# Attention of the hybrid layer in another order, with low parts and the gate on w_out's rows on VectorE

## The chip, the cores and the metric

One core of one Trainium2 chip runs the whole program. The metric is the device time of one execution in microseconds. Before the change three runs took 2250.26, 2250.78 and 2255.9 us; the median is 2250.78 us.

The engines are named as in the profile: PE multiplies, PEld loads its weights, DVE and ACT are the vector and the scalar engine, POOL is GpSimd, SP only issues transfers.

## What is computed

256 tokens of width 1024 pass two blocks (feed-forward, a mixing layer, feed-forward) and then one hybrid layer: a normed and modulated input, attention with two kinds of heads, an output product scaled by a gate, and 32 experts of which each token uses 4. The attention, cut to what the change touches:

```python
h = rms_norm_2(x, norm1_g) * (1.0 + scale1) + shift1
proj = h @ w_in                                  # six groups of 512 columns
aq, ak, av, bq, bk, bv = jnp.split(proj, IN_SPLITS, axis=-1)
aq, ak, bq, bk = (rms_norm_2(heads(t), g) for t, g in ...)   # per head of 64
o_a = dilated_mixture_attention(aq, ak, av, alibi_slopes(8)) # 8 heads of 64
# 4 heads, two score sets each, p = softmax(q k^T / 8 - slope * dist):
a = p[:, :, 0] - lam * p[:, :, 1]
o_b = rms_norm_2(a @ bv, diff_norm_g) * (1.0 - lambda_init)
mixed = jnp.concatenate([o_a, o_b], axis=-1) @ w_out
x = x + gate1 * mixed
h2 = rms_norm_2(x, norm2_g) * (1.0 + scale2) + shift2
return x + gate2 * moe_ffn(h2, ...)
```

## The kernel before

Every weight tile of the dense products is split into a high part, rounded by ACT, and a low part, the rest, which DVE subtracts (`split`, L198, tiles `wh` and `wl`). A product is then three: high by high, low by high, high by low.

A feed-forward ends with a "transition": while it finishes its last blocks, it loads and splits the first weights of what follows. There are six of these before the attention's end (`to_ffn` and `columns` in `run`, which pass POOL as the engine of the low parts): ffn1 to mixing and mixing to ffn2 in each layer, ffn2 to the next ffn1, and the last ffn2 to the attention. L329 to L331 make the gated value `gf` and its transpose `gT` for the second product of a feed-forward, L271 to L279 are the layer norm behind it, L868 to L874 the modulated norm `h` in front of the attention. In the mixing, L1763 makes the tile `Ut` which the next step of a recurrence multiplies, and L1785 and L1786 make its output `mix`.

`attention` multiplies the normed input by the six groups of columns of `w_in` (`natural`, 48 products of 128x512 for each, L412 to L414). Group 3 and 4 are q and k of the B heads, 5 their values, 0 and 1 q and k of the A heads, 2 their values. `qk` (L940 to L952) squares a group, sums per head, takes the inverse root by `rstd_wide` (ACT's logarithm and exponential, L236 and L237, and three small DVE operations), multiplies (L944) and transposes (L951, `turn`). `scores` (L967 to L978) makes the scores of one head, adds the bias and takes the maximum (L974), changes its sign (L975), takes exponentials with their sum (L977) and the reciprocal. `a_scores` divides by the sum (L995), `b_scores` combines two sets (L1013 to L1016). `transposed` (L984, L986) transposes the probabilities of one head on PE and copies them by ACT into a tile `eT`; `a_values` and `b_values` call it and multiply by the values at once (L1004, L1023). `b_values` also norms (L1027 to L1032), `b_turn` (L1037 to L1041) transposes the B heads' result.

What runs beside the columns is set by a list: `at(...)` appends a stage, and `beside` takes the next one after each half of `natural` and after each row block of `out_gemm`. Tiles wait for their buffers, and a scheduler may move instructions past each other on their engines where the program's data allow.

`out_gemm` multiplies by the rows of `w_out` (L574, 72 products, and L1082, 24). Before a row block is split, `scaled` multiplies it in place by the gate's row `g1` (L556, on POOL, tile `sq`), which POOL's queue loads (`mod_row`, L834).

The experts' weights, 192 pieces of 2 MB, come through nine slots in a fixed order (`moe_slots`); `prefetch` issues the next piece (L1252). One is issued at the attention's start, two by POOL's queue before `b_values(3)`, five in the route and one behind it. `route` chooses the experts after the attention; the first product of the experts is L1304.

## Time and profile before

| | |
|---|---|
| median of 3 runs | 2250.78 us |
| the profiled execution | 2255.59 us |
| its span | 2253.8 us |
| mean granted TensorE clock | 0.982 |
| PE busy | 2117.4 us (94% of the span) |
| DVE busy | 1094.1 us (49%) |
| ACT busy | 776.3 us (34%) |
| POOL busy | 155.0 us (7%) |
| moved by DMA | 637.66 MB, mean 283 GB/s |

The span runs from the first to the last instruction; the execution's time is a little longer. Busy shares are means over stages that differ: a stage is read from its own stretch, by what its engines waited for. The granted clock is a share of TensorE's full 2.4 GHz, and its lower level, 1.2 GHz, shows as 0.5.

### The profile page before, as it was taken

Reading aid. Unit: us, or ns where it says so; the run is one execution under the profiler, and the core shown is the slowest. Engines: PE = TensorE matmul, PEld = TensorE weight load, DVE = VectorE, ACT = ScalarE, POOL = GpSimd, SP = SyncE. Lnnn points to the kernel's source line nnn. Section 1 sums busy time; section 2 is a strip of 40 time slices with the busy share of each in tenths; the row PEclk is TensorE's granted clock in tenths of the full one; section 3 lists DMA queues with packets and bytes.
Section 4 is the critical chain, followed back from the end, with each engine's and each line's share of the span. In section 5 each row is a group of like instructions: output and inputs, shape, how many; then the busy total and the mean of one; then the engine's idle time right before and its main releaser. Section 6 shows DMA issues by size and latency. Waiting matters only on the chain.

```text
span 2253.8 us, 28233 instructions
## 1 busy us (share of the span) xinstructions
PE 2117.4 (94%) x11564; PEld 1355.5 (60%) x11565; DVE 1094.1 (49%) x1769; ACT 776.3 (34%) x1142; POOL 155.0 (7%) x160
## 2 busy tenths in 40 slices
PE   8999999999999999899989799999999999998997
PEld 7888777888788877688867563333332323232322
DVE  6766966876876686676676732121111111111111
ACT  4555742555455584245547520101010101010100
POOL 0002222000000122200020300000000000000000
PEclk9999998999999999999999799999999999999999
DMA  8765433776675543266554289999999999999996
GB/s 296 262 241 161 140 100 107 263 252 218 209 271 198 174 140 104 94 221 206 180 203 150 108 330 428 427 428 426 427 427 427 428 428 427 427 428 428 427 427 274
DMA packets 194437, 637.66 MB, mean 283 GB/s; under 512 B 25152, under 2 KB 133472, under 8 KB 169728
## 3 DMA queue, kind: packets, MB, share of 16 engines
q1 hardware_dynamic: 177488, 623.82, 70.9%
q0 software_dynamic: 2896, 9.88, 1.2%
q10 hardware_dynamic: 13920, 2.10, 0.5%
q8 instruction: 93, 1.52, 0.3%
q14 instruction: 40, 0.33, 0.0%
HBM read 633.91 MB, written 1.86 MB: 282 GB/s over the span
## 4 chain that ended last, share of the span: by engine, by line
PE 32%; DMA 23%; DVE 4%; ACT 2%; issue 1%; POOL 0%; SPq 0%; ACTq 0%; POOLq 0%
DMA rawm<-in_w_gate_up_dram 14%; PE w L1304 9%; PE w L1327 5%; DMA rawm<-in_w_down_dram 3%; DMA raw<-in_w_gate_up_dram 3%; PE w L161 3%; PE m L337 2%; DMA raw<-in_w_down_dram 2%; PE w L162 2%; PE w L1287 1%; PE w L574 1%; PE w L414 1%; PE w L412 1%; PE w L413 1%; PE w L1331 1%
## 5 line engine op out<-in xcount | busy, mean ns | idle before, releaser
L198 DVE TENSOR_TENSOR wl<-raw,wh 128x1024 fp32r<-128x1024 f32 x332 | 408.1, 1236 | 177.4 <-ACT wh L198 176.4
L198 ACT ACTIVATE wh<-raw 128x1024 fp32r<-128x1024 f32 (+1 forms) x350 | 365.9, 1050 | 328.6 <-PE w L161 109.6
L161 PE MATMUL w<-xT,wh 128*128 128x512 f32 x1328 | 470.5, 396 | 3.6 <-DVE ab L325 3.6
L1304 PE MATMUL w<-rawm,XT 128*64 128x512 f32 x1696 | 387.3, 599 | 22.5 <-DMA rawm<-in_w_gate_up_dram 21.3
L162 PE MATMUL w<-xT,wl 128*128 128x256 f32 x1328 | 374.1, 282 | 0.0
L161 PEld LDWEIGHTS w<-xT,wh 128*128 128x128 f32 x1328 | 250.9, 189 | 63.1 <-DVE ab L325 3.9
L1304 PEld LDWEIGHTS w<-rawm,XT 128*64 128x64 f32 x1696 | 113.9, 137 | 249.9 <-issue 200.8
L162 PEld LDWEIGHTS w<-xT,wl 128*128 128x128 f32 x1328 | 250.3, 188 | 1.6
L337 PE MATMUL m<-wh,gT 128*128 128x512 f32 x592 | 190.9, 393 | 0.0
L1327 PE MATMUL w<-rawm,wh 128*64 128x512 f32 x704 | 164.7, 599 | 14.2 <-DVE wh L1309 10.7
L1345 DVE COPY g<-w 128x64 f32<-128x64 f32 x32 | 7.1, 223 | 330.7 <-ACT PT L1343 330.7
L1352 DVE SCALAR_TENSOR_TENSOR wl<-w,gs,wh 128x512 f32<-128x512 f32 x31 | 23.3, 751 | 221.2 <-PE w L1327 221.2
L337 PEld LDWEIGHTS m<-wh,gT 128*128 128x128 f32 x592 | 111.1, 188 | 26.8 <-issue 1.7
L1327 PEld LDWEIGHTS w<-rawm,wh 128*64 128x64 f32 x704 | 46.3, 136 | 121.8 <-issue 88.8
L337 PE MATMUL m<-wl,gT 128*128 128x512 f32 x296 | 116.3, 393 | 0.0
L1318 ACT ACTIVATE wh<-w 128x512 f32<-128x512 f32 x32 | 19.1, 597 | 277.2 <-PE w L1317 277.2
L414 PE MATMUL w<-wh,xT 128*128 128x512 f32 (+1 forms) x224 | 87.4, 390 | 5.2 <-DVE xT L258 5.2
L1353 ACT ACTIVATE yh<-wl 128x512 fp32r<-128x512 f32 x31 | 19.5, 630 | 208.8 <-DVE wl L1352 208.8
L413 PE MATMUL w<-wl,xT 128*128 128x512 f32 (+1 forms) x224 | 87.3, 390 | 4.4 <-DVE wl L198 4.4
L412 PE MATMUL w<-wh,xT 128*128 128x512 f32 (+1 forms) x224 | 88.8, 398 | 2.5 <-ACT pre L739 1.9
L1304 PE MATMUL w<-raw,XT 128*64 128x512 f32 x352 | 80.3, 598 | 4.2 <-DMA raw<-in_w_gate_up_dram 3.6
L1327 PE MATMUL w<-raw,wh 128*64 128x512 f32 x320 | 75.6, 600 | 8.0 <-DVE wh L1309 5.3
(479 smaller groups left out, 2885.5 us busy)
## 6 DMA issues: line engine op xcount, KB each, us to landing
rawm<-in_w_gate_up_dram SPq DMA_DIRECT2D x104, 2048.0 KB
raw<-in_ffn_w_dram SPq DMA_DIRECT2D x130, 1024.0 KB
rawm<-in_w_down_dram SPq DMA_DIRECT2D x43, 2048.0 KB
raw<-in_w_gate_up_dram SPq DMA_DIRECT2D x22, 2048.0 KB
raw<-in_w_down_dram SPq DMA_DIRECT2D x20, 2048.0 KB
raw<-in_w_in_dram SPq DMA_DIRECT2D x36, 1024.0 KB
adaw<-in_w_ada_dram SPq DMA_DIRECT2D x48, 512.0 KB
raw<-in_w_out_dram SPq DMA_DIRECT2D x12, 1024.0 KB
```

The costliest lines, as they stand in the source:

```text
L161: nc.tensor.matmul(w[:, ab], h[:, k], self.xT[:, k], start=(k == 0), stop=False)
L162: nc.tensor.matmul(w[:, ab, :T], l[:, k], self.xT[:, k, :T], start=False, stop=(k == KD - 1))
L198: made = nc.scalar.activation(h, v, AF.Copy), (low or nc.vector).tensor_tensor(l, v, h.bitcast(F32), op=OP.subtract)
L337: mm = lambda g, w, start, stop: nc.tensor.matmul(acc[t][q], g, w[:, 0, q * 512 : (q + 1) * 512], start=start, stop=stop, skip_group_check ...
L412: self.nc.tensor.matmul(w[:, t, :n], xh, h, start=(k == 0), stop=False)
L413: self.nc.tensor.matmul(w[:, t, :n], xh, l, start=False, stop=False)
L414: self.nc.tensor.matmul(w[:, t, :n], xl, h, start=False, stop=(k == KD - 1))
L574: mm = lambda q, x, w, start, stop: nc.tensor.matmul(acc[t][:, q], x, w[:, 0, q * 512 : (q + 1) * 512], start=start, stop=stop, skip_group ...
L1287: nc.tensor.matmul(wv[:, k], h, at[:, t, lo:hi], start=(n == 0), stop=(n == 3))
L1304: nc.tensor.matmul(gu[c * 64 : c * 64 + 64, b], self.XT[:, k, e * 64 : e * 64 + 64], r[:, j, f0 : f0 + 512], start=False, stop=(k == KD - 1))
L1327: nc.tensor.matmul(td[c * 64 : c * 64 + 64], self.aT[:, s, q], r[:, s, c * 512 : (c + 1) * 512], start=(q == 0 and s == 0), stop=(q == 1 a ...
L1352: nc.vector.scalar_tensor_tensor(self.ms, td, self.gs, self.g2, op0=OP.mult, op1=OP.mult)
```

## The change

1. `scaled` multiplies on DVE instead of POOL.
2. The low parts of the six transitions are left to DVE, as all others.
3. In the attention PE keeps the order of the program (`manual_schedule`). The groups of columns come as 3, 4, 0, 1, 5, 2. Probabilities get a tile for each use and are transposed by `a_turn` and `b_probs_turn` one stage before the products that use them; `eT` gets a fourth buffer. The gate's row is loaded behind group 5.
4. The inverse roots in `qk` and `b_values` are taken by `rstd`: one small DVE operation (L225) and one power on POOL (L227, 128x16 and 128x2).
5. `scores` takes the smallest of the negated scores, and the exponential negates, so that the operation of L975 is gone.
6. One piece of the experts is issued before `b_values(3)` instead of two, and six in the route instead of five; the order of the slots changes in one place.

```diff
--- before.py
+++ after.py
@@ -553,7 +553,7 @@
-            self.nc.gpsimd.tensor_tensor(r[:, j], r[:, j], gain, op=OP.mult)
+            self.nc.vector.tensor_tensor(r[:, j], r[:, j], gain, op=OP.mult)
@@ -908,14 +908,19 @@
-            probs = [quarter(s3, i, 384) for i in range(4)]
-            osq = s3[:, 1536 : 1536 + T]
+            more = ap.tile([P, 384], F32, name="more")
+            probs = [quarter(s3, i, 384) for i in range(5)] + [more] + [quarter(s0, i, 384) for i in range(5)]
+            of_b = lambda hd: (probs[(0, 2, 3, 4)[hd]], probs[(1, 5)[hd % 2]])
+            of_a = lambda hd: probs[(6, 7, 8, 9, 10, 1, 5, 0)[hd]]
+            osq = lambda hd: quarter(s1, 4 + hd, T)
...
             self.prefetch(1)
+            order = self.tc.manual_schedule(engines={mybir.EngineType.PE})
+            order.__enter__()
             w3 = self.natural(None, 512, ahead)
...
-                r = self.rstd_wide(ap, ss, 1e-6, 1.0 / 64)
+                r = self.rstd(ap, ss, 1e-6, scale=1.0 / 64)
...
-            def scores(q, k, rows, p, bias):
+            def scores(q, k, rows, p, bias, s):
...
                 for t, c in parts:
-                    nc.vector.tensor_tensor_reduce(s[:, c], b[:, c], bias[:, c], 1.0, -3e38, OP.add, OP.max, m[:, t : t + 1])
-                nc.vector.tensor_scalar(m, m, -1.0, None, op0=OP.mult)
+                    nc.vector.tensor_tensor_reduce(s[:, c], b[:, c], bias[:, c], -1.0, 3e38, OP.add, OP.min, m[:, t : t + 1])
                 for t, c in parts:
-                    nc.scalar.activation(s[:, c], s[:, c], AF.Exp, bias=m[:, t : t + 1], accum_out=den[:, t : t + 1])
+                    nc.scalar.activation(s[:, c], s[:, c], AF.Exp, scale=-1.0, bias=m[:, t : t + 1], accum_out=den[:, t : t + 1])
...
-                eT = ap.tile([P, 384], F32, tag="eT", name=self.n("eT"), bufs=3)
+                eT = ap.tile([P, 384], F32, tag="eT", name=self.n("eT"), bufs=4)
...
+            def a_turn(p):
+                turned[p] = [transposed(kept["a", 2 * p + c]) for c in range(2)]
+
             def a_values(p):
-                eT = [transposed(kept[2 * p + c]) for c in range(2)]
+                eT = turned[p]
...
+            def b_probs_turn(hd):
+                turned["b", hd] = transposed(kept["b", hd])
+
             def b_values(hd):
-                eT = transposed(kept[hd])
+                eT = turned["b", hd]
...
-                r = self.rstd_wide(ap, ss, 1e-6, 1.0 / P)
+                r = self.rstd(ap, ss, 1e-6, scale=1.0 / P)
...
-            values(5, vb)
-            at((b_scores, 0)), at((b_scores, 1))
             w0 = self.natural([cols(0)], 512)
             qa, turn = qk(0, w0, 0)
-            at((b_values, 0), (b_scores, 2)), at((turn,), (b_values, 1))
+            at((b_scores, 0)), at((turn,), (b_scores, 1))
             w1 = self.natural([cols(1)], 512)
             ka, turn = qk(1, w1, 1)
-            at((b_scores, 3), (b_values, 2)), at((turn,))
+            at((b_scores, 2), (b_probs_turn, 0)), at((turn,), (b_scores, 3), (b_probs_turn, 1))
+            values(5, vb)
+            g1 = self.mod_row(scratch(), 2)
+            at((a_scores, 0), (b_values, 0), (b_probs_turn, 2), (b_values, 1))
+            at((b_probs_turn, 3), (a_scores, 1), (b_values, 2))
             va = values(2, [x[:, 512:] for x in ob])
-            self.prefetch(2, nc.gpsimd)
+            self.prefetch(1, nc.gpsimd)
+            a_turn(0)
             b_values(3)
-            a_scores(0)
+            a_scores(2)
+            a_values(0)
+            a_turn(1)
             b_turn(0)
             b_turn(1)
-            g1 = self.mod_row(scratch(), 2)
+            a_values(1)
             acc = [self.wide() for _ in range(2)]
-            at((a_scores, 1)), at((a_values, 0)), at((a_scores, 2)), at((a_values, 1), (a_scores, 3))
-            at((a_values, 2)), at((a_values, 3))
+            at((a_scores, 3)), at((a_turn, 2)), at((a_values, 2)), at((a_turn, 3)), at((a_values, 3))
...
+            order.__exit__(None, None, None)
@@ -1100,7 +1115,7 @@
-        self.prefetch(5)
+        self.prefetch(6)
@@ -1237,7 +1252,7 @@
-            for name in ("rawE", "xp", "slotp", "raw", "slotp", "raw", "raw2", "slotp", "raw2"):
+            for name in ("rawE", "xp", "raw", "slotp", "raw", "slotp", "raw2", "slotp", "raw2"):
@@ -1518,8 +1533,8 @@
-        to_ffn = lambda l, i: lambda: self.up_ahead(a[f"ffn{i}_w1"][l], a[f"ffn{i}_w3"][l], low=nc.gpsimd)
-        columns = lambda srcs, n: lambda: (None, (x for q in range(2) for x in self.natural_parts(srcs, n, q, nc.gpsimd)))
+        to_ffn = lambda l, i: lambda: self.up_ahead(a[f"ffn{i}_w1"][l], a[f"ffn{i}_w3"][l])
+        columns = lambda srcs, n: lambda: (None, (x for q in range(2) for x in self.natural_parts(srcs, n, q)))
```

The rows below are the engines' orders, before (or with -) and after (or with +), without times; line numbers of the changed kernel are up to 15 higher. First DVE at the transition to the attention, where `h_8550` is the modulated input of the first 128 tokens:

```order
 L872 TENSOR_TENSOR h_8550<-xn_146,row_8546 128x512 x2
+L198 TENSOR_TENSOR wl_10223<-raw,wh_10222 128x1024
+L225 TENSOR_SCALAR rs_e_10195<-mn_s_10193 128x1
+L198 TENSOR_TENSOR wl_10227<-raw,wh_10226 128x1024
+L874 SCALAR_TENSOR_TENSOR h_8550<-h_8550,rs_r_10197,row_8548 128x512 x2
 L271 BN_STATS st_10231<-m_8583 128x6
-L225 TENSOR_SCALAR rs_e_10195<-mn_s_10193 128x1
+L258 TENSOR_TENSOR xT<-m_10203,xT 128x4x128
+L258 TENSOR_TENSOR xT<-m_10210,xT 128x4x128
 L271 BN_STATS st_10231<-m_8584 128x6
-L874 SCALAR_TENSOR_TENSOR h_8550<-h_8550,rs_r_10197,row_8548 128x512 x2
```

Two low parts now stand between the two halves of the modulated norm, and the statistics of the other tokens follow it.

DVE before, around the first L995 and `b_turn` (L1041), where `slot_10277` holds probabilities of the A heads; POOL has eight L556 on its own queue:

```order
L995 TENSOR_SCALAR slot_10277<-slot_10277,st_10996 128x128
L995 TENSOR_SCALAR slot_10277<-slot_10277,st_10996 128x256
L978 RECIPROCAL st_11008<-st_11008 128x2
L974 ISA slot_10277,st_11061<-m_11058,biasA 128x256
L974 ISA st_11061 128x1
L995 TENSOR_SCALAR slot_10277<-slot_10277,st_11008 128x128
L995 TENSOR_SCALAR slot_10277<-slot_10277,st_11008 128x256
L1041 TENSOR_TENSOR slot_10278<-m_11017,slot_10278 128x4x128
L1041 TENSOR_TENSOR slot_10278<-m_11024,slot_10278 128x4x128
L975 TENSOR_SCALAR st_11061<-st_11061 128x2
L974 ISA slot_10277,st_11073<-m_11070,biasA 128x128
```

DVE after at the same place, behind the last group of columns (`m_10869` is a B head's result, `wl_11145` a low part of `w_out`, `m_10940` the scores of the A head 2):

```order
L556 TENSOR_TENSOR raw<-raw,sq_10811 128x1024
L1042 SCALAR_TENSOR_TENSOR h_8550<-m_10888,rs_r_10897,dg 128x128
L1042 SCALAR_TENSOR_TENSOR h_8551<-m_10888,rs_r_10897,dg 128x128
L556 TENSOR_TENSOR raw<-raw,sq_10811 128x1024
L198 TENSOR_TENSOR wl_11145<-raw,wh_11144 128x1024
L977 ISA slot_10276,st_10943<-m_10940,biasA 128x128
L977 ISA st_10943 128x1
L977 ISA slot_10276,st_10943<-m_10940,biasA 128x256
L977 ISA st_10943 128x1
L977 ISA slot_10276,st_10954<-m_10951,biasA 128x128
```

Two of the eight products by the gate and a low part stand ahead of the scores of A head 2.

PE before, behind `b_turn` (`m_11098` and `m_11104` are the transposes of pair 0 of the A heads, `eT_11102` the copy of the first, `w_11033` the first output of `w_out`):

```order
L984 MATMUL m_11098<-ident,slot_10277 128x128 x3
L984 MATMUL m_11104<-ident,slot_10277 128x128 x3
L1004 MATMUL m_11110<-eT_11102,h_8550 64x256
L1005 MATMUL m_11110<-eT_11102,h_8551 64x128
L1004 MATMUL m_11110<-eT_11108,h_8550 64x256
L1005 MATMUL m_11110<-eT_11108,h_8551 64x128
L967 MATMUL m_11136<-slot_10277 128x128
L968 MATMUL m_11136<-slot_10277 128x256
L967 MATMUL m_11148<-slot_10277 128x128
L968 MATMUL m_11148<-slot_10277 128x256
L984 MATMUL m_11176<-ident,slot_10277 128x128 x2
L574 MATMUL w_11033<-wh_11038,slot_10278 128x512
```

PE after, behind the last product of the columns (`m_10979` and `m_10985` are the transposes of pair 0 of the A heads, `eT_10983` the copy of the first, `m_10991` B head 3):

```order
L986 MATMUL m_10979<-ident,slot_10276 128x128 x3
L986 MATMUL m_10985<-ident,slot_10276 128x128 x3
L1033 MATMUL m_10991<-slot_10276,eT_10938 128x128
L1034 MATMUL m_10991<-slot_10276,eT_10938 128x128
L1035 MATMUL m_10991<-slot_10276,eT_10938 128x128
L972 MATMUL m_11004<-slot_10277 128x128
L973 MATMUL m_11004<-slot_10277 128x256
L972 MATMUL m_11015<-slot_10277 128x128
L973 MATMUL m_11015<-slot_10277 128x256
L1011 MATMUL m_11026<-eT_10983,h_8550 64x256
L1012 MATMUL m_11026<-eT_10983,h_8551 64x128
L1011 MATMUL m_11026<-eT_10989,h_8550 64x256
```

In the first, a head's transposes and its values follow each other; in the second, a B head's values and the scores of pair 2 stand between a pair's transposes and its values.

## Rows read from the trace of the kernel before

**Rows 1.** Busy time by stretch (us, busy of PE, PEld, DVE, ACT, POOL; PEclk, DMA, GB/s)

```profile
0.00:1166.30 1166.30, 1108.64 (x6514) 940.56 (x6515) 835.77 (x1212) 593.13 (x816) 134.28 (x148) 0.98 0.56 192
1166.30:1242.70 76.40, 73.30 (x345) 57.52 (x346) 51.09 (x133) 56.14 (x95) 0.00 (x0) 0.98 0.47 164
1242.70:1272.20 29.50, 14.46 (x69) 8.68 (x67) 24.52 (x53) 17.38 (x42) 19.63 (x10) 0.66 0.23 89
1272.20:1303.70 31.50, 31.06 (x143) 23.77 (x144) 18.09 (x47) 11.38 (x27) 0.56 (x1) 0.94 0.55 206
1303.70:1330.00 26.30, 25.55 (x164) 19.75 (x164) 12.76 (x40) 9.70 (x17) 0.55 (x1) 0.81 0.70 259
1330.00:2240.00 910.00, 858.02 (x4304) 302.65 (x4302) 149.28 (x282) 87.01 (x143) 0.00 (x0) 1.00 1.00 422
```

**Rows 2.** Timeline of SP's queue, 1304 to 1335: start, length, instruction

```profile
1317.93 12.17 SPq L1252 DMA_DIRECT2D rawm<-in_w_down_dram  x2
```

**Rows 3.** What PE waited for, 1166 to 1305: us, times, longest

```profile
PE m L984 <- DVE slot L995: 7.3, 4, 2.5
PE m L1023 <- ACT eT L986: 4.6, 3, 1.6
PE w L574 <- DVE wl L198: 4.0, 1, 4.0
PE m L967 <- DVE st L974: 1.9, 1, 1.9
```

**Rows 4.** Timeline of POOL, 1250 to 1275

```profile
1252.52 18.58 POOL L556 TENSOR_TENSOR raw<-raw,sq 128x1024 f32<-128x1024 f32 x8 [7.70 <-DMA sq<-mods]
```

**Rows 5.** DVE's groups, 1250 to 1275: busy us, mean ns

```profile
L995 DVE TENSOR_SCALAR slot<-slot,st 128x128 f32<-128x128 f32 (+1 forms) x8 | 9.9, 1277 | 0.0
L975 DVE TENSOR_SCALAR st<-st 128x2 f32<-128x2 f32 x5 | 5.5, 1096 | 0.0
L198 DVE TENSOR_TENSOR wl<-raw,wh 128x1024 fp32r<-128x1024 f32 x2 | 4.4, 2222 | 0.0
```

**Rows 6.** Timeline of DVE, the same operations undisturbed

```profile
1250.09 0.16 DVE L975 TENSOR_SCALAR st<-st 128x2 f32<-128x2 f32 x1
1251.82 0.55 DVE L995 TENSOR_SCALAR slot<-slot,st 128x128 f32<-128x128 f32 x2
1272.97 1.21 DVE L198 TENSOR_TENSOR wl<-raw,wh 128x1024 fp32r<-128x1024 f32 x1
```

**Rows 7.** Timeline of PE, two successive products in full flow

```profile
1240.87 0.39 PE L413 MATMUL w<-wl,xT 128*128 128x512 f32 x1
1241.10 0.39 PE L414 MATMUL w<-wh,xT 128*128 128x512 f32 x1
```

**Rows 8.** ACT's groups by form, 1166 to 1305

```profile
L236 ACT ACT_TABLE_LOAD x7 | 9.0, 1283 | 0.1
```

**Rows 9.** POOL's groups by form, whole span

```profile
L227 POOL TENSOR_TENSOR rs_r<-rs_e,mhalf 128x8 f32<-128x8 f32 x4 | 6.6, 1657 | 26.1 <-DVE rs_e L225 26.1
```

**Rows 10.** Timeline of DVE, last ffn2 into attention

```profile
1143.86 3.55 DVE L279 SCALAR_TENSOR_TENSOR xn<-y,rs_r,ln_b 128x512 f32<-128x512 f32 x2
1147.33 3.43 DVE L872 TENSOR_TENSOR h<-xn,row 128x512 f32<-128x512 f32 x2
1150.69 0.68 DVE L271 BATCH_NORM_STATS2 st<-m 128x6 f32<-128x512 f32 x1
1158.13 1.29 DVE L872 TENSOR_TENSOR h<-xn,row 128x512 f32<-128x512 f32 x2
```

**Rows 11.** What PE waited for, 1120 to 1167

```profile
PE m L252 <- DVE h L874: 6.2, 2, 6.0
PE m L337 <- ACT gT L330: 1.5, 1, 1.5
```

**Rows 12.** What PE waited for, 340 to 600

```profile
PE m L337 <- ACT gT L330: 2.7, 1, 2.7
```

**Rows 13.** What PE waited for, 900 to 945 (second mixing into ffn2)

```profile
PE m L1767 <- DVE Ut L1763: 1.7, 1, 1.7
```

More of the change, by code (lines that the diff above doesn't have):

```diff
@@ L968, in scores @@
                 nc.tensor.matmul(b[:, P:384], q[rows, p, P:T], k[rows, p, 0:T], start=True, stop=True)
-                s = probs.pop(0)
-                probs.append(s)
                 st = ap.tile([P, 4], F32, tag="st", name=self.n("st"), bufs=8)
@@ L992, in a_scores @@
                 for hd in (2 * p, 2 * p + 1):
-                    s, den = scores(qa, ka, slice(hd % 2 * 64, hd % 2 * 64 + 64), p, self.biasA[:, hd])
+                    s, den = scores(qa, ka, slice(hd % 2 * 64, hd % 2 * 64 + 64), p, self.biasA[:, hd], of_a(hd))
                     for t, cs in parts:
                         nc.vector.tensor_scalar(s[:, cs], s[:, cs], den[:, t : t + 1], None, op0=OP.mult)
-                    kept[hd] = s
+                    kept["a", hd] = s
+            turned = {}
+            def a_turn(p):
+                turned[p] = [transposed(kept["a", 2 * p + c]) for c in range(2)]
             def a_values(p):
-                eT = [transposed(kept[2 * p + c]) for c in range(2)]
+                eT = turned[p]
                 o = self.bank()
@@ L1010, in b_scores @@
             def b_scores(hd):
-                s0, d0 = scores(qb, kb, slice(0, 64), hd, self.biasB[:, hd])
-                s1, d1 = scores(qb, kb, slice(64, 128), hd, self.biasB[:, hd])
+                s0, d0 = scores(qb, kb, slice(0, 64), hd, self.biasB[:, hd], of_b(hd)[0])
+                s1, d1 = scores(qb, kb, slice(64, 128), hd, self.biasB[:, hd], of_b(hd)[1])
                 nc.vector.tensor_scalar(d1, d1, nlam, None, op0=OP.mult)
@@ L1016, in b_scores @@
                     nc.vector.scalar_tensor_tensor(s0[:, cs], s1[:, cs], d1[:, t : t + 1], s0[:, cs], op0=OP.mult, op1=OP.add)
-                kept[hd] = s0
+                kept["b", hd] = s0
+            def b_probs_turn(hd):
+                turned["b", hd] = transposed(kept["b", hd])
             def b_values(hd):
-                eT = transposed(kept[hd])
+                eT = turned["b", hd]
                 o = self.bank()
@@ L1026, in b_values @@
                 oc = slice(hd * P, (hd + 1) * P)
-                nc.scalar.activation(osq, o[:, :T], AF.Square)
+                nc.scalar.activation(osq(hd), o[:, :T], AF.Square)
                 ss = ap.tile([P, 2], F32, tag="oss", name=self.n("oss"), bufs=2)
-                nc.vector.tensor_reduce(ss, osq.rearrange("p (t i) -> p t i", t=2), AX.X, OP.add)
-                r = self.rstd_wide(ap, ss, 1e-6, 1.0 / P)
+                nc.vector.tensor_reduce(ss, osq(hd).rearrange("p (t i) -> p t i", t=2), AX.X, OP.add)
+                r = self.rstd(ap, ss, 1e-6, scale=1.0 / P)
                 for t in range(2):
```

## The prediction

> **What bounds the kernel now.** I read the table by stretches first [rows 1]. From 1330 to 2240 us the DMA share is 1.00 at 422 GB/s: the weights of the 32 experts stream in, in 192 pieces of 2 MB. Nothing before that fills the DMA (0.47, 0.23, 0.55 in the attention, 0.70 in the route). So the end hangs on when the stream begins without a break. Nine pieces are issued ahead; the row of the last of them [rows 2] holds two issues, and the second one, the tenth piece, ends at 1330.1: it needs a buffer which the first expert's products give free, and these follow the route, 26 us after the attention's last product (L1082, 1303.7). From there to the end nothing changes. Hence the rule of this prediction: a microsecond of the attention, or of anything before it, is one of the end, as long as the nine pieces have landed when the first expert wants them.
>
> Before 1166 PE is busy 1108.6 of 1166.3 us at a granted clock of 0.98 [rows 1]: PE is the bound there, and only its waits can be had. The attention is three stretches [rows 1]: A (1166.3 to 1242.7, the columns of `w_in`; PE busy 73.3 of 76.4), B (to 1272.2, from the last of these columns to where `w_out`'s products run without a break; PE busy 14.5 of 29.5, DVE 24.5, the granted clock 0.66, between the two levels of 2.4 and 1.2 GHz) and C (to 1303.7; PE busy 31.1 of 31.5).
>
> The chain of PE's waits in there [rows 3] names DVE's L995 (7.3 us), its low part L198 (4.0) and L974 (1.9), all in B, and ACT's L986 (4.6 in three waits, two of them in A).
>
> **Why B is slow.** POOL multiplies `w_out`'s rows by the gate from 1252.5 on, eight in a row, 18.6 us, after 7.7 us of waiting for the gate's row [rows 4]. In that time DVE's operations that read SBUF last several times what they last elsewhere: eight L995 9.9 us, five L975 5.5, two L198 4.4 [rows 5]; undisturbed a pair of L995 takes 0.55, an L975 0.16, an L198 1.21 [rows 6]. So 9.9 - 2.2, 5.5 - 0.8 and 4.4 - 2.4 is lost: 7.7 + 4.7 + 2.0 = 14.4 us of DVE's 24.5. L974, which reads PSUM and one SBUF tile, is not drawn out.
>
> The Trainium skill's page "SBUF — State Buffer", section "Who interferes with whom", says that a DVE instruction with two SBUF inputs, or in a two-port mode, contends with a GpSimd instruction that reads SBUF, and that the second to come blocks for the whole of the other. The stretched L198 and L995 agree with it; by the page the whole 14.4 us would go with the move to DVE, as by the rows.
>
> **The change, part by part.**
>
> *Gate on DVE.* POOL's 18.6 us go. DVE takes eight operations of the shape of L198 (128x1024, two SBUF inputs), so 1.21 each [rows 6], 9.7 in all. By the order, two of them stand before the end of the last columns, ahead of a low part that those need; three in B and three in C. The gate's row is now requested behind w1's power, by my setting of the order some 15 us before the end of A, and the low part behind the first gate is wanted some 10 us after that; today's load costs POOL 7.7 us of waiting [rows 4], so it fits, by little.
>
> *B after.* DVE's own work there: 24.5 - 14.4 = 10.1; plus three gates (3.6), plus low parts, of which the order has three in B where one and a half stood (1.8), less the scores of heads 0 and 1 that move into A (about 1.7): 14 us. The order also has a chain: PE's first products of head pair 0 wait for ACT's copy of the transposed probabilities, which stands behind ACT's exponentials of pair 1, which wait for DVE's L974 of pair 1, which stands behind two gates and a low part. That chain costs waits that are not DVE work; I put 4 us on it. B after is 18 us (from 14, DVE without a wait, to 24.5, all of DVE's busy time of now), a gain of 11.5 (5 to 15.5).
>
> *C after.* The 96 products of `w_out` (8 row blocks, 2 x 2 outputs, 3 terms) at 0.23 us (two successive starts [rows 7]) are 22 us, with the last scores, transposes and values of the A heads, some 4 us, 26. Today it is 31.5 with a first part at the lower clock and the 4.0 us wait in front of it as B's last [rows 3]. If the clock is down at the start, because PE waits in B, some 1.5 us come on top: 27.5, a gain of 4.0 (1.5 to 5.5).
>
> *A after.* The two L986 waits (3.1 of 4.6) arise as ACT does two table loads for each root, 14 in the attention, 1.28 us each for L236 [rows 8] and as many for L237, with the copy behind them. The root is now one POOL power per use. For the 128x16 case the trace has only 128x8, at 1.66 us [rows 9]: between that and twice it, 3.3; I take 3. DVE's product L944 waits for it, as it now waits for ACT's two loads, two functions and three small DVE operations (about 3.5), so the wait itself is no longer than before. Behind L944 stand low parts for the next columns; the last one comes a little late for w0 and w1 (0.4 us each, by setting the order against 11.2 us of products). Into A move the transposes of w1's columns and the scores of pair 0, about 2 us of PE work that B loses. So A gains 3.1 - 0.8 - 2.0, near 0.5 (a loss of 1 to a gain of 3). Program order on PE changes nothing there: its columns ran in that order already.
>
> *The smaller edits.* Sixteen L975 (0.16 us undisturbed) leave DVE; hidden behind PE everywhere but B, and counted there. More buffers for probabilities and a fourth eT take no time. One piece fewer is fetched before the end of the attention and one more by the route: by the order of SP's queue five pieces then follow from about 1270 on, 4.9 us each at the stream's 422 GB/s, the last before the route needs it. Free, covered by the DMA's share of 0.55 in C [rows 1]; 4.9 us if the cover fails.
>
> *Low parts of the six transitions.* At the step to the attention, POOL's low parts draw L279 out to 3.55 us a pair and L872 to 3.43, where a pair of L872 takes 1.29 later [rows 10]; with L279 taken as like it, 4.4 us go. PE's wait for `gT` there (1.5 [rows 11]) goes as well. Against it: two low parts of 1.21 now stand between L872 and L874, and two L271 (0.68 [rows 10]) follow L874 that lay beside POOL's work. 1.5 + 4.4 - 2.4 - 1.4: a gain near 2.0. At the step from ffn2 to the next ffn1 the wait for `gT` (2.7 [rows 12]) is down to about 0.6: 2.1. At each step from mixing to ffn2 a low part now stands in front of L1786 and so of `Ut` (L1763), for which PE waits 1.7 us [rows 13]: it waits 1.2 us longer, twice, a loss of 2.4. The steps from ffn1 to mixing (576 columns) have room. Net 1.7 (a loss of 2.4 to a gain of 5).
>
> **Sum.** 0.5 + 11.5 + 4.0 + 1.7 = 17.7 us. The profiled execution takes 2255.6 (span 2253.8), the median of the three runs is 2250.78 and two of them lie at 2250.3 and 2250.8, so the profiled one is 4.8 above. The gain is the same for both: 2237.9 on the profiled one's scale, 2233 on the median's.
>
> **The rivals.**
>
> *B's chain stays as long.* DVE has 9.7 us more to do and PE now may not go past a late instruction. If B lasts 29.5 and C starts as cold as now, only A and the transitions gain: 2250.8 - 2.2 = 2248.6, no change. For it: the chain above crosses ACT and DVE three times. Against it: it needs 15 us of waits beside 14 of work.
>
> *The powers lock DVE.* By the page's rule above, POOL's power reads SBUF and would block a low part (two SBUF inputs) as the gate does now. By the rows, the price is a power's length each time a low part stands between the root's input and L944. The order shows that once (w1) of four times, since L944 mostly follows at once: 3.3 us; if all four block, 13.2. 2236 to 2246. Against it: three of the four have only L944 behind them, which waits for its power in any case.
>
> *A piece comes late.* With one piece fewer ahead the first experts catch up with the DMA: 4.9 us, 2238. Against it: 26 us of route at a share of 0.70.
>
> *Slower: the columns run at the lower clock.* The last low part of w0, w1 and w2 stands behind a DVE product that waits for a power. If that wait grows to several microseconds in front of each, PE idles as in B, and there the granted clock was 0.66. At 1.2 GHz 48 products take 11.2 us more. Three times that is 33.6: 2233 + 33.6 = 2267. It turns the gain into a loss over 0.3% once 2.2 of the three are cold (17.7 + 6.8 = 24.5 over 11.2). Against it: A's clock is 0.98 with waits of 1.6 us in it [rows 1, 3].
>
> **How the numbers follow.** Forecast 0.66 (own range 2222 to 2241), chain as long 0.13, powers 0.06, late piece 0.09, cold columns 0.06. A difference under 0.3%, 6.8 us, is about what cannot be told from none. Faster needs less than 2244.0: 0.66 less 0.02, 0.09, 0.05 of the powers, and 0.05 of the first rival, where only C gains: 0.83. Within: 0.11. Slower: 0.06. The range of 2219 to 2247 leaves out most of the first rival and the cold columns above, and at the low end what B and the transitions would bring together at their bounds.
>
> **What would show it.** After: no POOL instruction of 128x1024; L995 pairs at 0.55 throughout; no table loads between `exp` calls; B (from the last column product to unbroken `w_out` products) near 18 us, C near 27.5, A near 76; two waits for `Ut` of 2.9; PE's wait for h (L874) near 3 where it is 6.2 [rows 11]; the first expert's tenth piece issued 17 to 18 us sooner. It is wrong if B is above 25, if a low part behind L944 holds PE over 2 us in A, or if the stream of weights starts with a gap.

## The result and the profile after

The changed kernel takes 2226.14 us, the median of four runs (2224.84 to 2233.84), against 2250.79 for four of the kernel before: 0.9893, 95% interval 0.9866 to 0.9919, so 24.6 us or 1.1% less. Forecast were 2233, a range of 2219 to 2247, and faster at 0.83. Direction and range hold; the gain is 7 us larger than the sum.

Single runs of one kernel lie up to 16 us apart here (11 of the kernel before, on one chip: 2247.6 to 2263.4). So below the lengths of stretches are compared, with medians beside them: A, B and C together last 115.4 and 114.7 us in two profiles of the changed kernel, 137.2 in that of before and in that of E3, whose attention is the same.

The profiled execution takes 2226.42 us, its span 2224.6. The busy table by stretch, cut where [rows 1] is cut, with the same columns:

```profile
0.00:1162.00 1162.00, 1110.51 (x6514) 942.48 (x6515) 842.41 (x1230) 592.65 (x816) 99.11 (x129) 0.98 0.56 192
1162.00:1238.40 76.40, 75.61 (x357) 59.42 (x358) 54.62 (x124) 43.95 (x82) 15.33 (x7) 0.96 0.43 145
1238.40:1250.10 11.70, 8.73 (x68) 6.22 (x66) 11.12 (x41) 9.40 (x30) 1.98 (x3) 1.00 0.85 325
1250.10:1277.30 27.20, 26.92 (x134) 20.50 (x133) 16.81 (x38) 10.14 (x22) 0.56 (x1) 1.00 0.65 249
1277.30:1300.50 23.20, 22.48 (x163) 17.22 (x163) 12.94 (x41) 9.71 (x17) 0.56 (x1) 0.93 0.79 298
1300.50:2210.00 909.50, 857.48 (x4301) 302.48 (x4298) 149.40 (x282) 87.00 (x143) 0.00 (x0) 1.00 1.00 423
```

Against [rows 1]: the attention begins at 1162.0 instead of 1166.3. A lasts 76.4 as before, though with PE busy 75.6 of it instead of 73.3. B lasts 11.7 instead of 29.5, with the clock at 1.00 instead of 0.66. C lasts 27.2 instead of 31.5. The route, here 23.2 instead of 26.3, is the same code; its clock was 0.81 before and is 0.93 now. That difference is scatter: from the attention's last product to the first one of the experts (L1304 before, L1319 after) it is 21.2 us before and 18.0 after, but 17.9 and 18.1 in E9 and E3, whose attention is as slow as before, and 17.8 to 20.1 in all others. From there to the last work of the engines it is 923.1 us before and 923.2 after. What PE waited for, 1120 to 1305 (to compare with [rows 3, 11]):

```profile
PE m L252 <- DVE h L874: 5.0, 2, 3.1
PE w L414 <- DVE xT L258: 2.0, 1, 2.0
PE m L986 <- DVE h L1042: 0.9, 1, 0.9
PE m L1033 <- DVE st L977: 0.8, 1, 0.8
PE m L972 <- ACT eT L988: 0.7, 1, 0.7
```

Of the four waits in [rows 3] none over 0.9 us is left; what stays at the attention's begin is 2.0 for xT, and the wait for h (L874) has gone from 6.0 to 3.1 at its longest. DVE's groups inside B now:

```profile
L198 DVE TENSOR_TENSOR wl<-raw,wh 128x1024 fp32r<-128x1024 f32 x2 | 2.4, 1220 | 0.0
L556 DVE TENSOR_TENSOR raw<-raw,sq 128x1024 f32<-128x1024 f32 x2 | 2.4, 1218 | 0.0
L997 DVE TENSOR_SCALAR slot<-slot,st 128x128 f32<-128x128 f32 (+1 forms) x6 | 1.5, 312 | 0.0
```

L198 and the gate's L556 take 1.22 us each, one after the other on DVE, and L997 (before: L995) 0.31 where it took 1.28 in [rows 5]. DVE is busy 11.12 of B's 11.70 us, ACT 9.40 and PE 8.73: by busy time DVE is the nearest to the limit now.

### The profile page after: what moved, and what is told of

Same layout as the page of the kernel before. It is cut to its first block, busy times and chain, and to the rows that moved or that the text cites. A ratio compares the mean times of both kernels' runs of the same rounds, so it can differ in the third digit from the quotient of the medians.

```text
span 2224.6 us, 28162 instructions
## 1 busy us (share of the span) xinstructions
PE 2108.9 (95%) x11564; PEld 1351.2 (61%) x11565; DVE 1089.9 (49%) x1755; ACT 754.4 (34%) x1112; POOL 117.5 (5%) x141
## 4 chain that ended last, share of the span: by engine, by line
PE 33%; DMA 26%; DVE 3%; ACT 1%; issue 0%; POOL 0%; SPq 0%; ACTq 0%; POOLq 0%
DMA rawm<-in_w_gate_up_dram 14%; PE w L1319 8%; DMA rawm<-in_w_down_dram 5%; PE w L1342 5%; DMA raw<-in_w_gate_up_dram 4%; PE w L161 3%; PE m L337 2%; DMA raw<-in_w_down_dram 2%; PE w L162 2%; PE w L574 1%; PE w L1302 1%; PE w L414 1%; PE w L413 1%; PE w L412 1%; PE w L1346 1%; PE m L1378 1%
## 5 line engine op out<-in xcount | busy, mean ns | idle before, releaser
L198 DVE TENSOR_TENSOR wl<-raw,wh 128x1024 fp32r<-128x1024 f32 (+1 forms) x350 | 422.8, 1216 | 187.8 <-ACT wh L198 186.9
L198 ACT ACTIVATE wh<-raw 128x1024 fp32r<-128x1024 f32 (+1 forms) x350 | 366.3, 1051 | 346.4 <-PE w L161 113.3
L1319 PE MATMUL w<-rawm,XT 128*64 128x512 f32 x1536 | 351.1, 599 | 20.9 <-DMA rawm<-in_w_gate_up_dram 19.9
L1319 PEld LDWEIGHTS w<-rawm,XT 128*64 128x64 f32 x1536 | 103.1, 137 | 222.0 <-issue 179.4
L1342 PE MATMUL w<-rawm,wh 128*64 128x512 f32 x848 | 197.6, 599 | 15.5 <-DVE wh L1324 12.0
L1342 PEld LDWEIGHTS w<-rawm,wh 128*64 128x64 f32 x848 | 55.7, 136 | 142.5 <-issue 102.7
L1319 PE MATMUL w<-raw,XT 128*64 128x512 f32 x512 | 116.7, 598 | 5.7 <-DMA raw<-in_w_gate_up_dram 5.0
L1319 PEld LDWEIGHTS w<-raw,XT 128*64 128x64 f32 x512 | 34.3, 136 | 76.2 <-issue 61.8
```

The source lines that it names most:

```text
L198: made = nc.scalar.activation(h, v, AF.Copy), (low or nc.vector).tensor_tensor(l, v, h.bitcast(F32), op=OP.subtract)
L1319: nc.tensor.matmul(gu[c * 64 : c * 64 + 64, b], self.XT[:, k, e * 64 : e * 64 + 64], r[:, j, f0 : f0 + 512], start=False, stop=(k == KD - 1))
L1342: nc.tensor.matmul(td[c * 64 : c * 64 + 64], self.aT[:, s, q], r[:, s, c * 512 : (c + 1) * 512], start=(q == 0 and s == 0), stop=(q == 1 a ...
```

## The experiments

Lengths in us, from the start of products in each profile: A from the first column product behind the wait for xT to the end of the last one, B and C together from there to the end of the last product of `w_out`. In E11 that wait is gone, so only B and C can be set beside the others. The medians in the first two rows are those of the result.

| kernel | A | B + C | sum | median | ratio to before, 95% |
|---|---|---|---|---|---|
| before | 76.4 | 60.8 | 137.2 | 2250.8 | |
| after | 76.4 | 39.0 | 115.4 | 2226.1 | 0.9893 (0.9866 to 0.9919) |
| E1 before, gate on DVE | 76.3 | 51.1 | 127.4 | 2246.7 | 0.9972 (0.9957 to 0.9987) |
| E2 after, gate on POOL | 78.9 | 46.0 | 124.9 | 2237.0 | 0.9919 (0.9900 to 0.9937) |
| E3 before, low parts on DVE | 76.4 | 60.8 | 137.2 | 2249.4 | 0.9975 (0.9960 to 0.9989) |
| E4 after, low parts on POOL | 74.7 | 39.0 | 113.7 | 2234.3 | 0.9906 (0.9885 to 0.9926) |
| E5 after, again | 75.2 | 39.5 | 114.7 | 2230.2 | 0.9872 (0.9848 to 0.9897) |
| E6 after, roots by ACT | 76.1 | 48.4 | 124.5 | 2235.8 | 0.9913 (0.9888 to 0.9938) |
| E7 after, PE free | 76.1 | 40.5 | 116.6 | 2228.3 | 0.9866 (0.9838 to 0.9893) |
| E8 after, five pieces in the route | 74.9 | 40.3 | 115.2 | 2226.7 | 0.9871 (0.9845 to 0.9896) |
| E9 before, roots by POOL | 76.1 | 60.6 | 136.7 | 2257.5 | 1.0011 (0.9999 to 1.0023) |
| E10 before, all but the order | 76.0 | 49.2 | 125.2 | 2236.2 | 0.9932 (0.9910 to 0.9955) |
| E11 after, L822 later | | 39.0 | | 2222.7 | 0.9867 (0.9845 to 0.9888) |

Beside E1 to E4 the kernel before had a median of 2254.6, beside E5 to E8 2257.8, beside E9 to E11 2254.4.

**E1, E2: the gate's products.** The edit, in the kernel before and reversed in the changed one:

```diff
-            self.nc.gpsimd.tensor_tensor(r[:, j], r[:, j], gain, op=OP.mult)
+            self.nc.vector.tensor_tensor(r[:, j], r[:, j], gain, op=OP.mult)
```

> The kernel before, with the eight products by the gate (L556) on DVE and nothing else changed. Theory (POOL's products block DVE): the stretch B, 29.5 us before, loses the 14.4 us by which DVE's operations were drawn out and takes on some four products of 1.2 us, so it lasts 18 to 21 us, and the median goes from 2250.8 to about 2241. Rival (the order of transposes and values makes B long, not the block): B stays above 26 us and the median within 3 us of 2250.8.

> The changed kernel, with the eight products by the gate back on POOL and nothing else. Theory of the block: DVE's operations with two SBUF inputs beside them are drawn out to 2 to 4 us again, B goes from 11.7 to above 20 us and the median from 2226 to 2235 or more. Rival (the new order alone hides them): B stays under 15 us, the median within 3 us of 2226.

With the gate on DVE the attention is 9.8 us shorter in the old order (E1); with it on POOL it is 9.5 longer in the new one (E2). The median of E1 falls by 7.9, where 10 were expected, and its rival (within 3) falls. In E1 no single stretch can be set against B's forecast, since products of `w_out` and waits alternate there; B and C together lose 9.7. E2's rival falls too: its ratio stands 0.0026 and 0.0047 behind the two of the changed kernel (E5 is the second), 6 to 11 us. Its first product of `w_out` starts 19.4 us behind A's end, just short of the 20 expected, and 2.5 of its 9.5 us lie in A, where POOL now begins. E2's POOL (one row of eight products), then DVE's groups beside it:

```profile
1222.93 21.52 POOL L556 TENSOR_TENSOR raw<-raw,sq 128x1024 f32<-128x1024 f32 x8 [3.64 <-DMA sq<-mods]
```

```profile
L997 DVE TENSOR_SCALAR slot<-slot,st 128x128 f32<-128x128 f32 (+1 forms) x12 | 11.2, 983 | 0.1
L198 DVE TENSOR_TENSOR wl<-raw,wh 128x1024 fp32r<-128x1024 f32 x4 | 7.0, 1746 | 3.4 <-ACT wh L198 3.4
```

L997 is back at 0.98 on average instead of 0.31, L198 at 1.75 instead of 1.22. While POOL multiplies, each tensor_scalar of DVE takes about as long as one of POOL's products, some 2.3 us. The prediction says this of DVE's operations that read SBUF, but it isn't so for all of them: the reduction L1039 and the reciprocal L980 read SBUF too and keep their 0.40 and 0.14 us. DVE in E2, two rows of its timeline and one of its groups while POOL multiplies (1223 to 1244.4):

```profile
1233.22 9.03 DVE L997 TENSOR_SCALAR slot<-slot,st 128x128 f32<-128x128 f32 x4
1242.17 2.30 DVE L225 TENSOR_SCALAR rs_e<-oss 128x2 f32<-128x2 f32 x1
```

```profile
L1039 DVE TENSOR_REDUCE oss<-slot 128x2 f32<-128x256 f32 x2 | 0.8, 400 | 0.0
```

POOL's eight products last 21.5 us there, and 18.6 in [rows 4]: five take 2.3 to 2.4 us each, as all eight do before, and three take 3.2 to 3.4. That fits DVE holding POOL up too. What PE waited for in E2:

```profile
PE m L972 <- DVE h L1042: 6.6, 1, 6.6
PE m L1033 <- DVE st L977: 3.0, 1, 3.0
```

The longest, 6.6 us, is for the B heads' result (L1042), not for probabilities. Behind it are two causes that E2 doesn't separate: the L225 above, the input of that head's root, is held until 1244.5, and the root's power stands behind the eight products on POOL's own queue, which end at 1244.5 as well. E1 takes the attention's roots on ACT, so its 9.8 us are those of the products alone.

**E3, E4: the low parts of the transitions.**

```diff
-        to_ffn = lambda l, i: lambda: self.up_ahead(a[f"ffn{i}_w1"][l], a[f"ffn{i}_w3"][l], low=nc.gpsimd)
+        to_ffn = lambda l, i: lambda: self.up_ahead(a[f"ffn{i}_w1"][l], a[f"ffn{i}_w3"][l])
...
-        columns = lambda srcs, n: lambda: (None, (x for q in range(2) for x in self.natural_parts(srcs, n, q, nc.gpsimd)))
+        columns = lambda srcs, n: lambda: (None, (x for q in range(2) for x in self.natural_parts(srcs, n, q)))
```

> The kernel before, with the low parts of the six transitions on DVE and nothing else. The two profiles show the attention begin 4.4 us sooner after the change (1162.0 for 1166.3): theory, the transitions give 3 to 5 us, the median is 2246 to 2248. Rival, the prediction's own sum: 1.7 us, 2249. A third: the two runs merely differ, and the transitions give nothing.

> The changed kernel, with the low parts of the six transitions back on POOL and nothing else. Theory: the attention begins near 1166 again, the median is 2229 to 2231, and PE's wait for Ut falls back to 1.7 us while that for h (L874) rises from 3.1 to 6. Rival, the prediction's own sum: 2228. A third: no difference from 2226.

E3 gains 5.2 us on the medians (2.5 to 9.0 by its interval), so the forecast of 1.7 just falls, and so does "nothing". E4's ratio stands 0.0013 and 0.0034 behind the two of the changed kernel, 3 to 8 us, but the intervals overlap. Its waits are as expected, 1.7 for `Ut` and 6.0 for h. Its attention begins at 1167.3 where the changed kernel's begins at 1162.0, but this begin scatters: 1155.1 to 1166.0 in the nine profiles with these low parts on DVE (1165.1 in E3), 1166.3 to 1169.3 in the four with them on POOL.

Where the gain comes from is seen by setting the same PE products of the profiles side by side. At the step to the attention, between 1130 and 1155, all nine profiles with these low parts on DVE gain 4.7 to 5.4 us on the profile of before, and E1, E4 and E9 nothing; by the second half of the first columns some 3 are left. At the step from ffn2 to the next ffn1, between 550 and 600, eight of the nine gain 1.1 to 1.7 (E8 loses 1.0), and E1, E4 and E9 lose 1.6 to 3.3. At the step from mixing to ffn2 the wait for `Ut` rises as forecast, 340 to 600 in the profile after:

```profile
PE m L1782 <- DVE Ut L1778: 3.0, 1, 3.0
PE m L337 <- ACT gT L330: 1.0, 1, 1.0
```

3.0 for the 1.7 of [rows 13], the same at both such steps, and `gT` 1.0 for the 2.7 of [rows 12]. But within 40 us the lateness at the first `Ut` is given back: between 345 and 400 the shift against before changes by -0.8 in the changed kernel and in E3, by -0.9 in E1 and E4, whose low parts are on POOL (-1.8 to 1.3 in the other profiles with them on DVE, -3.1 in E9). At the second one, between 920 and 945, profiles with the low parts on DVE fall back by 0 to 1.2 us, the one after by 3.0, and E1, E4 and E9 by 0.9, -1.2 and 0.8. So of the loss of 2.4 in the sum about 1 may be there, and it can't be told from scatter.

**E5: the changed kernel again.**

> The changed kernel itself once more, beside the kernel before, since runs of one kernel lie up to 10 us apart here. Theory: the stretches A, B and C together last 115.4 us again (before 137.2), and what scatters lies in the mixing, in the route and where the experts' stream begins; the median is 2222 to 2230 with before at 2250 to 2255.

114.7 for 115.4, and 2230.2 at the upper end of the range, beside 2257.8 for the kernel before, above its own. The ratio repeats (0.9872 for 0.9893). The experts' part, from its first product to the last work of the engines, lasts 927.7 in this profile and 923.2 in the first one: 4.5 us of scatter that the change doesn't make, since E9, with the old attention, has 928.7.

**E6: the roots by ACT again.**

```diff
-                r = self.rstd(ap, ss, 1e-6, scale=1.0 / 64)
+                r = self.rstd_wide(ap, ss, 1e-6, 1.0 / 64)
...
-                r = self.rstd(ap, ss, 1e-6, scale=1.0 / P)
+                r = self.rstd_wide(ap, ss, 1e-6, 1.0 / P)
```

> The changed kernel, with the inverse roots of the attention by ACT's logarithm and exponential again (two table loads each) and nothing else. Theory (the loads hold up the copies and the exponentials behind them on ACT): A gains 2 to 4 us and B, whose chain crosses ACT three times and holds four roots, 2 to 5; the median rises by 4 to 9 over the changed kernel. Rival, the prediction's sum: a root by ACT takes 3.5 us where a power takes 3, so A and B together rise by no more than 2, as the transposes now stand a stage ahead.

9.1 us more, all of it in B and C, none in A: the place of the theory is half right, and B, 9.6 longer than after, is above its upper bound of 5. The median is 5.7 above that of E5 beside it, inside the theory's 4 to 9, and the rival falls. The row of B in E6's busy table, and ACT's loads for the logarithm inside it:

```profile
1231.20:1252.50 21.30, 13.85 (x68) 10.36 (x66) 13.57 (x58) 18.71 (x42) 0.53 (x1) 0.68 0.54 197
```

```profile
L236 ACT ACT_TABLE_LOAD x3 | 3.8, 1283 | 0.1
```

B lasts 21.3 us with ACT busy 18.7 of them, and with as many loads at L237 six loads take 7.7 us. DVE is busy 13.6. With the roots by ACT it is ACT that is nearest to the limit in B, as without them it is DVE; and the granted clock is 0.68, about as in B before (0.66).

**E7: PE in the scheduler's order.**

```diff
-            order = self.tc.manual_schedule(engines={mybir.EngineType.PE})
-            order.__enter__()
...
-            order.__exit__(None, None, None)
```

> The changed kernel without the program's order on PE: the scheduler may again move PE's instructions. Theory (the order in which the steps are written makes the gain): A, B and C stay within 2 us of 115.4 together and the median within 3 us of the changed kernel. Rival (program order keeps products from standing in front of late probabilities): transposes and values slip among the products of w_out again, B or C grow by 4 us or more.

116.6 for 115.4, and no ratio that tells them apart: holding PE to program order is worth nothing that these runs show. What is left of part 3 of the change is the order in which the steps are written, with its buffers.

**E8: the pieces ahead.**

```diff
-        self.prefetch(6)
+        self.prefetch(5)
```

> The changed kernel, with five pieces of the experts' weights issued in the route instead of six, so eight ahead in all. Theory (the pieces ahead are covered, the stream's end hangs on the first buffer that comes free): the next piece is issued by the experts' first steps and the time from the first expert's product to the end stays at 923 us, the median within 3 us. Rival (each piece ahead is worth its own 4.9 us on a full DMA): 4 to 5 us more.

The time from the first expert's product to the end is 923.3. The edit took no piece away, though: the experts' first step asks for it, at 1283.46 by SP's timeline, seven microseconds after the attention's end, where the changed kernel issues it right at that end:

```profile
1283.46 0.52 SPq L1267 DMA_DIRECT2D rawm<-in_w_gate_up_dram  x1
```

What it shows is that a piece may come that much later at no cost, not what a missing one costs.

**E9, E10: the roots in the old order, and everything but the order.** E9 is the kernel before with E6's edit reversed; E10 has that, E1's edit and E3's.

> The kernel before, with the inverse roots by POOL's power and nothing else (the gate's products stay on POOL). Theory (in the old order B ends with POOL's eight products whatever the roots do): the roots gain the 3.1 us of PE's waits in A at most, A, B and C together go from 137.2 to 133 or more. Rival (the roots are worth the same 9 us in either order): 128, and the median 9 us below the kernel before.

> The kernel before, with the gate on DVE, the low parts on DVE and the roots by POOL's power, but the old order of groups, transposes and buffers. If the parts add up (gate 9.6, roots 9.1 of the 21.8 us), A, B and C together last 118 us, 3 more than in the changed kernel, and the order is worth 3 us. Rival (the new order is what lets the others pay): 124 or more. A third: the order is worth nothing, 115.

E9 gains 0.5 us in the attention and nothing in time: the first theory. POOL's eight products and DVE's groups beside them, in E9:

```profile
1256.20 19.64 POOL L556 TENSOR_TENSOR raw<-raw,sq 128x1024 f32<-128x1024 f32 x8 [4.31 <-DMA sq<-mods]
```

```profile
L995 DVE TENSOR_SCALAR slot<-slot,st 128x128 f32<-128x128 f32 (+1 forms) x8 | 10.7, 1374 | 0.0
L198 DVE TENSOR_TENSOR wl<-raw,wh 128x1024 fp32r<-128x1024 f32 x3 | 6.5, 2167 | 0.0
```

As long as POOL blocks DVE, the unbroken products of `w_out` start behind POOL's last one, and the loads taken off ACT buy 0.5 us. E10 lasts 125.2, as long as E6 and E2: the parts do not add up, and the rival holds. What PE waited for in E10:

```profile
PE m L1023 <- ACT eT L986: 4.2, 2, 2.7
PE w L414 <- DVE xT L258: 2.8, 1, 2.8
PE w L574 <- DVE w L264: 1.5, 1, 1.5
PE m L1004 <- ACT eT L986: 1.1, 1, 1.1
```

With gate and roots moved, the old order still has products that wait for ACT's copy of the transposes right in front of them (L1023, L1004: 5.3 us, of which 2.7 in A), and B and C lose 10.2 against the changed kernel. These waits are the smaller part of it. B and C as one stretch, in E10 and after:

```profile
1235.80:1285.00 49.20, 42.33 (x210) 29.79 (x209) 36.12 (x101) 25.61 (x62) 3.07 (x5) 0.97 0.40 144
1238.40:1277.30 38.90, 35.65 (x200) 26.72 (x199) 27.94 (x77) 19.55 (x51) 2.54 (x4) 1.00 0.71 272
```

Behind the columns the old order has 8.2 us more of DVE's work, 6.1 of ACT's and 6.7 of PE's busy time, and 3.6 more in which PE is idle. In A the changed kernel has 6.0 us more of DVE's work than E10 (54.6 for 48.6): the new order moves work from behind the columns to beside them, where PE is busy anyway. E10 differs from the changed kernel in the small edits too (sixteen L975 of 0.16 us, the pieces of the experts, PE's program order), so the 9.8 us are the order's with these. The order alone in the kernel before was not run.

**E11: an edit that the profile after suggests.** In front of the second half of the first columns DVE has L822, a product that nobody needs until the route, and waits there for a transfer (DVE's timeline after):

```profile
1160.09 1.23 DVE L822 SCALAR_TENSOR_TENSOR row<-row,sq 128x1024 f32<-128x1024 f32 x1 [2.13 <-DMA row<-mods]
1161.23 1.28 DVE L258 TENSOR_TENSOR xT<-m,xT 128x512 fp32r<-128x512 f32 x2
```

```diff
-        self.nc.vector.scalar_tensor_tensor(A, A, 1.0, scratch, op0=OP.add, op1=OP.mult)
+        made = self.nc.vector.scalar_tensor_tensor(A, A, 1.0, scratch, op0=OP.add, op1=OP.mult)
+        if name == "norm2_g_2":
+            self.tc.keep_in_program_order(made)
...
+            next(gain2)
             kb, turn = qk(4, w4, 3)
             at(), at((turn,))
-            next(gain2)
```

> The changed kernel, with the product L822 (the second norm's row, which waits for a transfer) kept behind the low parts of the first columns on DVE, where the profile shows it 2.1 us waiting in front of the last xT. Theory: PE's wait of 2.0 us for xT goes and the second half of the first columns starts 2 to 3 us sooner, so 2 to 3 us off the changed kernel's median. Rival: the wait moves to the power of the first root, behind which L822 now stands, and nothing is gained.

The same operations in E11, then the power beside L822:

```profile
1158.60 1.36 DVE L258 TENSOR_TENSOR xT<-m,xT 128x512 fp32r<-128x512 f32 x2 [0.71 <-ACT xT L257]
1168.22 1.22 DVE L822 SCALAR_TENSOR_TENSOR row<-row,sq 128x1024 f32<-128x1024 f32 x1
```

```profile
1168.40 3.83 POOL L227 TENSOR_TENSOR rs_r<-rs_e,mhalf 128x16 f32<-128x16 f32 x1 [9.70 <-DVE rs_e L225]
```

xT (L258) starts at 1158.6 instead of 1161.2. The granted clock from 1160 to 1170, after and in E11:

```profile
1160.00:1170.00 10.00, 8.03 (x22) 6.29 (x23) 4.97 (x6) 3.18 (x3) 0.00 (x0) 0.59 0.10 43
```

```profile
1160.00:1170.00 10.00, 10.00 (x45) 8.04 (x44) 7.41 (x11) 6.07 (x6) 1.60 (x1) 1.00 0.52 158
```

From the start of the second tokens' L872 (L874 in E11; 1153.7 and 1153.6) to the end of the attention it is 123.8 us after and 118.4 in E11, 5.4 less, and 4.9 less than in E5 (123.3). Of the 5.4, 2.9 lie in front of the second half of the columns, where the wait was, and 2.6 in A, whose clock stayed at its upper level instead of 0.59. Its median is the lowest of the study (2222.7), but E7's ratio (0.9866) is as low as its 0.9867, and its interval overlaps those of the changed kernel, so as a time it is not shown to be faster. The rival's wait is there, and hidden: the power next to L822 takes 3.8 us instead of 2.9.

## Why the prediction was right, and by how much its terms were not

**What bounds the kernel.** Right. The experts' part lasts 923.2 us for 923.1, and the end moved by what the attention and the stages before it gained (26 us in these two profiles), with the scatter of the route (3 us) on top. The tenth piece is issued at 1300.4 instead of 1329.7, so the stream moved as the end did, by 29 us in these two profiles.

**A** (gain 0.5, bounds -1 to 3): 0.0 in these two profiles. The waits for L986 are gone (3.1), and PE is busy 2.3 us more with the work that moved in. Part of A is how long the clock stays at its lower level behind the wait for xT, and that scatters between two profiles of the changed kernel. The first ten microseconds of A, after and in E5, where the wait is 2.8 us:

```profile
1162.00:1167.00 5.00, 5.00 (x12) 3.94 (x13) 1.74 (x2) 1.42 (x2) 0.00 (x0) 0.50 0.00 0
1167.00:1172.00 5.00, 5.00 (x22) 3.94 (x21) 3.32 (x7) 3.56 (x4) 0.00 (x0) 0.88 0.36 109
1162.10:1167.10 5.00, 5.00 (x15) 3.96 (x16) 1.88 (x3) 2.12 (x2) 0.00 (x0) 0.66 0.00 0
1167.10:1172.10 5.00, 5.00 (x24) 3.98 (x23) 4.45 (x8) 3.04 (x3) 0.00 (x0) 1.00 0.53 174
```

In E5 A lasts 75.2 us, a gain of 1.2.

**B** (gain 11.5, bounds 5 to 15.5): 17.8, outside the bounds. This is the mis-sized term, 6.3 us. The forecast had 14 us of DVE work and 4 us of waits in the chain over ACT; measured are 11.1 of work, since two products by the gate and two low parts lie in B where three of each were counted, and 0.6 of DVE's idle time. The 4 us of waits for the chain were not there. What was wrong below the number is its cause. The sum gave nearly the whole gain of B to the gate's products, and put the roots into A and at nothing in B. E1 and E2 show 9.6 for the gate; E6 shows 9.1 for the roots, in B, where ACT otherwise spends 7.7 us in loads; E10 shows 9.8 for the order with the small edits. Each of the three, taken out of the changed kernel, leaves the attention at 124.5 to 125.2. In the kernel before, the gate alone gives 9.8 and the roots alone 0.5. So the stretch behind the columns has three limits that lie close together: DVE with POOL's block, ACT with its loads, and the work that the old order leaves there. With all three edits in, removing one brings back the full 9 to 10 us. That the time fell inside the range was in part luck: B came out beyond its bounds, by the roots, which the sum had at nothing there, and by the work that the order moves away, which it had at 1.7 us. The forecast of 18 us for B lies near what is measured with the roots left on ACT (E6, 21.3).

**C** (gain 4.0): 4.3, with the clock at 1.00 in B and in C, so the 1.5 us charged for a cold start did not arise; the work itself is 27.2 us where 26 were counted, and the two errors nearly cancel.

**Transitions** (gain 1.7, bounds -2.4 to 5): 5.2 in E3, with an interval of 2.5 to 9.0; the 4.3 between the first two profiles is within the scatter of the attention's begin. The step to the attention gives more than 2.0 (5 at its middle, some 3 behind it), and of the 2.4 us charged for `Ut` at least the first half is given back within 40 us: a wait on PE was taken for a loss of the end, without asking what absorbs it.

**The rivals.** B's chain as long: no, except with one of the three undone. The powers lock DVE: the lock exists, and the other way round. POOL's powers after:

```profile
1196.40 2.90 POOL L227 TENSOR_TENSOR rs_r<-rs_e,mhalf 128x16 f32<-128x16 f32 x1 [9.35 <-DVE rs_e L225]
1210.51 3.74 POOL L227 TENSOR_TENSOR rs_r<-rs_e,mhalf 128x16 f32<-128x16 f32 x1 [11.21 <-DVE rs_e L225]
1236.53 1.54 POOL L227 TENSOR_TENSOR rs_r<-rs_e,mhalf 128x2 f32<-128x2 f32 x1 [0.86 <-DVE rs_e L225]
```

A 128x16 power takes 2.90, so the prediction's 3 held. The second row is w1's, behind whose input a low part stands, on DVE's timeline after:

```profile
1210.28 1.22 DVE L198 TENSOR_TENSOR wl<-raw,wh 128x1024 fp32r<-128x1024 f32 x1
```

DVE's operation begins 0.23 us ahead of the power and takes its 1.22 us undisturbed; the power takes 3.74, 0.84 more. The rival's price, 3.3 us of DVE, was not paid. The last row, a 128x2 power, meets a product by the gate: 1.54, where others of its shape take 0.70 to 0.71. POOL was held up, and no operation of DVE that the profile after shows beside a power of the attention was drawn out. By the Trainium skill, "SBUF — State Buffer", section "Who interferes with whom", the one that comes first holds the ports and the other blocks; the trace agrees, with 0.84 us of waiting behind the 1.0 us that DVE's operation still ran. A late piece: none seen. Cold columns: the clock is 0.96 in A, and its lower level is behind the wait for xT alone.

Of the signs that were named, A, C, both waits for `Ut` and the one for h came as said; B (11.7 for 18) and the tenth piece (29 us sooner for 17 to 18) did not, both on the side of more gain.

## What to carry to other kernels

Where a stretch is longer than PE's work in it, count the work of every engine there, not only of the one that the waits name: here three limits lay close together. An edit which gains 0.5 us by itself (the roots, E9) can be worth 9 us once the other limits are gone, so take parts out of the finished version as well as putting them into the old one. A wait which grows costs only what nothing behind it gives back; follow it to the next place where PE waits anyway.

## What was not expected of the hardware

POOL's eight products took 18.6 us in the kernel before, 19.6 in E9 and 21.5 in E2, with different work of DVE beside them. That the block also runs the other way, and costs a power 0.84 us next to one operation of DVE, was not in the prediction. And behind PE's wait of 2.0 us for xT the granted clock was at its lower level, 0.50, for five microseconds and still 0.88 in the next five (changed kernel), while in E5, behind a longer wait of 2.8 us at the same place, it was 0.66 and 1.00; in E11, without the wait, it was 1.00 from 1160 to 1170. What sets the length of that spell these runs don't show.
